# Output stage in two phases: all merges by 512 tokens, then the last projection by Strassen's block product

## The chip, the cores and the metric

One core of one Trainium2 chip runs the whole program. The metric is the time of one execution on the device, in microseconds. TensorE (PE) multiplies matrices into PSUM; VectorE (DVE), ScalarE (ACT) and GpSimd (POOL) work on SBUF tiles of 128 partitions, and SyncE (SP) issues most DMA transfers. Each engine runs its instructions in the order in which they were fixed when the program was built, and waits for the others by semaphores.

## The reference

One layer with two mixers in parallel over 2048 latent tokens of width 1024, in fp32. The change lies in what follows the mixers:

```
ya = rmsnorm(oa, gla_onorm).reshape(b, t, GLA_V) * jax.nn.silu(ag)
yb = rmsnorm(ob, gdn_onorm).reshape(b, t, GDN_V) * jax.nn.silu(bg)
gates = jax.nn.sigmoid(mg + b_gate.astype(jnp.float32))
merged = gates[..., :D_MODEL] * jnp.matmul(ya, w_gla_out) + gates[..., D_MODEL:] * jnp.matmul(yb, w_gdn_out)
out_x = jnp.matmul(merged, w_o)
...
x = x + (gt_x[:, None, :] * out_x).astype(dtype)
return rmsnorm(x, final_g)
```

`ya` and `yb` are 2048 x 512 each, `w_gla_out` and `w_gdn_out` 512 x 1024, `w_o` 1024 x 1024.

## The kernel before

**Products.** An fp32 operand is kept as two tiles of the type fp32r, a rounded half `h` and the rest `l`. `split` makes them: a cast on ScalarE (L132) and a subtraction on VectorE or GpSimd (L135, after the argument `lo`). A product is three matmuls for each 128 rows of depth: h·h, h·l and l·h.

**Blocks.** The latent tokens are 8 blocks of 256 (two tiles of 128), finished by the scans in the order 3, 4, 2, 5, 1, 6, 0, 7. Gated mixer outputs lie in DRAM as `d_y`, gates as `d_gate`. The output stage has two parts for each block.

`out_merge(b)` (from L1579) makes `merged` for 256 tokens, transposed: for each of 8 column tiles j, 12 matmuls of 128 x 256 for either mixer into the two halves of one PSUM bank `pm` (L1592), 192 a block. VectorE then computes (stored gate + 1) · pm (L1596), adds the two mixers (L1598), and `split` makes `mh` (ScalarE) and `ml` (VectorE). Its weights `wab` are split in `out_weights`; the raw tiles `wr` come from a ring of four.

`phase_out` (from L1603) does the last projection: for each token tile and half of the 1024 columns 24 matmuls of 128 x 512 into `pz` (L1661), 96 a block, against `wo`, the whole of `w_o` in halves, in SBUF. Then VectorE multiplies by `gtb` (L1666), GpSimd adds x (L1667), and ScalarE squares and sums (L1668). `flush` finishes a tile a little later: the inverse root on GpSimd (L1631, L155, L156), the scaling on VectorE (L1635), and the store (L1637). The y of the next block is loaded and split (`out_y`, on ScalarE and GpSimd) while a block's projection runs.

**What sets the order.** The code calls `out_merge` and the projection by turns, block by block; the build keeps each engine's order by data dependences and its priorities. For block 3, the weights and merges are woven into the last step of the scans (`phase_mix`, L1519 to L1521), together with that step's remaining matmuls (L1409 among them); `w_o` is split there and in the first block's projection. PSUM has two banks for `pm`; `mt`, the tile behind a merge and a projection, is one buffer.

## Time and profile before

| | |
|---|---|
| runs, us | 2157.18, 2164.18, 2164.04 (median 2164.04) |
| profiled execution's own time, us | 2161.12 |
| its span in the profile, us | 2159.3 |
| granted TensorE clock over the span | 0.989 |
| output stage alone, from the end of the scans' matmuls, us of the span | 1813.4 to 2159.3 |

The span is the time from the first to the last instruction that the profile shows; the execution's own time holds what lies around it as well. Lines named L1592 and the like are lines of the kernel before unless the text says that they are of the changed one. In rows of the trace `out<-in` gives the tiles by the program's names, then the shape, and in brackets how long the engine had been idle and what ended that.

### The profile page before, as it was taken

Reading aid. Unit: us, or ns where it says so; the run is one execution under the profiler, and the core shown is the slowest. Engines: PE = TensorE matmul, PEld = TensorE weight load, DVE = VectorE, ACT = ScalarE, POOL = GpSimd, SP = SyncE. Lnnn points to the kernel's source line nnn. Section 1 sums busy time; section 2 is a strip of 40 time slices with the busy share of each in tenths; the row PEclk is TensorE's granted clock in tenths of the full one; section 3 lists DMA queues with packets and bytes.
Section 4 is the critical chain, followed back from the end, with each engine's and each line's share of the span. In section 5 each row is a group of like instructions: output and inputs, shape, how many; then the busy total and the mean of one; then the engine's idle time right before and its main releaser. Section 6 shows DMA issues by size and latency. Waiting matters only on the chain.

```text
span 2159.3 us, 41811 instructions
## 1 busy us (share of the span) xinstructions
PE 2062.3 (96%) x16096; PEld 1730.3 (80%) x16096; DVE 1215.5 (56%) x2185; ACT 899.0 (42%) x2212; POOL 858.6 (40%) x779
## 2 busy tenths in 40 slices
PE   5999999999999999999999999899988888999998
PEld 2688888888888888777777777788888777999888
DVE  3813555556777553556555555566677776444333
ACT  4644255555452223443434443355555554112111
POOL 2410122222221015666666663456566664222331
...
GB/s 288 104 86 116 50 69 64 63 62 72 61 62 80 71 80 133 138 138 152 143 127 148 128 142 140 262 286 292 308 281 288 285 212 273 130 134 114 98 88 79
DMA packets 275012, 315.60 MB, mean 146 GB/s; under 512 B 22280, under 2 KB 206844, under 8 KB 274812
## 3 DMA queue, kind: packets, MB, share of 16 engines
...
q14 instruction: 73, 0.60, 0.1%
HBM read 203.00 MB, written 109.84 MB: 145 GB/s over the span
## 4 chain that ended last, share of the span: by engine, by line
PE 82%; DVE 5%; ACT 5%; DMA 3%; POOL 2%; issue 2%; SPq 1%; DVEq 0%; POOLq 0%; ACTq 0%
PE pz L371 46%; PE pz L1661 8%; PE pm L1592 8%; DMA g<-dg 2%; PE pe L936 1%; PE pe L1118 1%; PE pl L995 1%; PE pl L988 1%; PE pl L996 1%; PE pz L1080 1%; DVE ql L1215 1%; ACT E L1209 1%; PE pz L1059 1%; PE pq L614 1%; PE pz L1347 1%
## 5 line engine op out<-in xcount | busy, mean ns | idle before, releaser
L371 PE MATMUL pz<-hi,wh 128*128 128x512 f32 (+1 forms) x1560 | 621.6, 399 | 1.5 <-DVE hi L134 1.5
L371 PE MATMUL pz<-lo,wh 128*128 128x512 f32 (+1 forms) x1560 | 600.3, 385 | 1.8 <-POOL lo L135 1.8
L371 PE MATMUL pz<-hi,wl 128*128 128x512 f32 (+1 forms) x1520 | 588.4, 387 | 0.0
L371 PEld LDWEIGHTS pz<-lo,wh 128*128 128x128 f32 x1560 | 294.7, 189 | 51.0 <-POOL lo L135 3.6
L371 PEld LDWEIGHTS pz<-hi,wh 128*128 128x128 f32 x1560 | 294.3, 189 | 47.8 <-DVE hi L134 2.4
L371 PEld LDWEIGHTS pz<-hi,wl 128*128 128x128 f32 x1520 | 286.1, 188 | 53.9 <-issue 0.4
L135 POOL TENSOR_TENSOR wl<-w,wh 128x1024 fp32r<-128x1024 f32 x44 | 110.0, 2500 | 437.5 <-ACT wh L132 312.0
L569 DVE SCALAR_TENSOR_TENSOR acc<-zpad,cw,acc 128x1024 f32<-128x1024 f32 x192 | 272.3, 1418 | 6.6
L1592 PE MATMUL pm<-yh,wab 128*128 128x256 f32 x1024 | 188.2, 285 | 2.2 <-ACT fsq L1402 1.4
L873 DVE CAST_PREDICATED U<-kit,pl 128x256 f16<-128x256 int32 x216 | 91.1, 431 | 139.2 <-PE pl L996 135.4
L1592 PEld LDWEIGHTS pm<-yh,wab 128*128 128x128 f32 x1024 | 161.8, 193 | 3.1 <-ACT fsq L1402 1.6
L1661 PE MATMUL pz<-wo,mh 128*128 128x512 f32 (+1 forms) x528 | 161.3, 388 | 0.0
L1592 PE MATMUL pm<-yl,wab 128*128 128x256 f32 x512 | 145.5, 284 | 0.0
L989 ACT CAST ppb<-pl 128x256 f16<-128x256 f32 x216 | 73.5, 373 | 166.7 <-PE pl L988 160.3
L1216 POOL TENSOR_TENSOR E<-E,ak 128x256 f32<-128x256 f32 x96 | 78.9, 841 | 110.6 <-ACT E L1209 67.0
L1661 PEld LDWEIGHTS pz<-wo,mh 128*128 128x128 f32 x528 | 98.2, 189 | 20.1
L135 DVE TENSOR_TENSOR sql<-sq,sqh 128x512 fp32r<-128x512 f32 (+1 forms) x36 | 28.0, 804 | 140.5 <-ACT sqh L132 140.2
L624 POOL TENSOR_TENSOR acc<-acc,sq 128x512 f32<-128x512 f32 x32 | 50.6, 1586 | 137.7 <-ACT sq L623 77.7
L1661 PE MATMUL pz<-wo,ml 128*128 128x512 f32 (+1 forms) x264 | 102.0, 386 | 0.0
L1592 PEld LDWEIGHTS pm<-yl,wab 128*128 128x128 f32 x512 | 98.9, 193 | 0.3
L135 POOL TENSOR_TENSOR yl<-wr,yh 128x1024 fp32r<-128x1024 f32 x16 | 39.2, 2462 | 128.2 <-ACT yh L132 128.2
L1666 DVE TENSOR_TENSOR mt<-pz,gtb 128x512 f32<-128x512 f32 (+1 forms) x33 | 22.3, 675 | 115.3 <-PE pz L1661 113.1
...
## 6 DMA issues: line engine op xcount, KB each, us to landing
...
dqkv<-acc SPq DMA_DIRECT2D x192, 64.0 KB, 1.6
...
```

The lines of the kernel that those rows point to most:

```text
L135: getattr(nc, lo).tensor_tensor(dst_lo, src, dst_hi.bitcast(F32), op=ALU.subtract)
L371: nc.tensor.matmul(ps[:, 0:n], a[:, kk, :], b[:, kk, :], start=(k == 0), stop=(k == last - 1))
L569: nc.vector.scalar_tensor_tensor(acc, src, wcol, acc, op0=ALU.mult, op1=ALU.add)
L614: nc.tensor.matmul(u[4][:, 0:u[2]], self.ones, u[3][i], start=(i == 0), stop=(i == 1))
L624: nc.gpsimd.tensor_tensor(v, v, r, op=ALU.mult)
L873: self.nc.vector.copy_predicated(out, mv, data)
L936: nc.tensor.matmul(ps[:, o + a * P:o + 256], qk[:, 1, h, :], kq[:, h, a:2, :], start=True, stop=True)
L989: nc.scalar.copy(ppl, pc.rearrange("p h (j i) -> p h j i", i=m))
L1216: nc.gpsimd.tensor_tensor(E[:, :, li, 1], E[:, :, li, 1], k, op=ALU.mult)
L1592: nc.tensor.matmul(ps[:, half * 256:half * 256 + 256], wab[wi][:, k, j * P:(j + 1) * P], yy[:, k, :], start=(i == 0), stop=(i == 11))
L1661: nc.tensor.matmul(ps, aa[:, k, i * P:(i + 1) * P], wo[k][wi][:, cs], start=(j == 0), stop=(j == 23))
L1666: nc.vector.tensor_tensor(sq, ps, gtb[:, cs], op=ALU.mult)
```

## The change

The output stage becomes two phases.

*Merges first.* Blocks are taken in four groups of two (`groups`), and each merge matmul moves 512 tokens (L1597 of the changed kernel, 192 a group). The product with the gate is now one L1600 for each mixer, then one addition (L1604); the result is stored to DRAM (`d_m`, L1605), with no split. The group's y are four tiles (hi and lo for each mixer). `out_weights` keeps `wab` in four pairs of columns.

*w_o.* It is no longer kept whole. During the last merge group and after it, `wo_block` makes seven blocks of 512 x 512 in halves: B11, B21 and B22 themselves, T1 = B12 - B11, T3 = B22 - B12 (one subtraction, L1624), T2 = B22 - T1 and T4 = B21 - T2 (two subtractions, of the hi and of the lo half, L1629).

*The product.* Each block of 256 tokens by 1024 is cut into A11 to A22 (128 tokens by 512). `m_raws` reads it back, `m_sums` makes S1 = A21 + A22, S2 = S1 - A11, S3 = A22 - S2, S4 = A12 - S2 on VectorE (L1643), and `m_halves` splits each left operand (cast on ScalarE; subtraction on VectorE for even products, on GpSimd for odd ones; four buffers). Seven products of 12 matmuls of 128 x 512 (L1738) replace 96 matmuls with 84. Products 2, 4 and 6 (counted from 0) accumulate onto the bank of product 0, product 5 onto that of product 1. ScalarE copies the bank after products 0, 1, 2 and 4 (L1743); VectorE (L1752, L1758) and GpSimd (L1755) add what makes the four quarters of the output. `fin` does what followed the projection before (L1725 on VectorE, L1726 on GpSimd, L1727 on ScalarE), four times a block, and `flush` the end of a tile (L1704, L155, L156 on GpSimd, L1708 on VectorE). The sums and splits of the next block's first three products are made during products 4 to 6.

```diff
-NW = 6
...
+PRODUCTS = (("A11", "B11"), ("S1", "T1"), ("S2", "T2"), ("A12", "B21"), ("S3", "T3"), ("S4", "B22"), ("A22", "T4"))
...
+        self.d_m = dp.tile([NLAT // 2, P, 8, 256], F32, name="dm")
...
-                gens.append((itertools.chain(self.out_weights(), self.out_merge(self.blocks[0])), 10))
+                gens.append((itertools.chain(self.out_weights(), self.out_merge(0)), 10))
...
-    blocks = (3, 4, 2, 5, 1, 6, 0, 7)
+    groups = ((3, 4), (2, 5), (1, 6), (0, 7))
 
     def out_open(self):
-        wp = self.pool("owa", 1, side="right")
-        self.yp = self.pool("oy", 1, side="right")
-        self.sp = self.pool("os", 2, side="right")
+        self.bp = self.pool("ob", 1, side="right")
+        self.sp = self.pool("os", 3, side="right")
         self.pm = self.pool("opm", 2, PSUM, side="right")
-        self.wab = [wp.tile([P, 8, D], F32R, name=f"wab{i}") for i in range(2)]
+        self.wab = [[self.w_blk().rearrange("p a b -> p (a b)").rearrange("p (k n) -> p k n", k=8) for _ in range(2)]
+                    for _ in range(4)]
...
-    LO = ("vector", "gpsimd") * 7 + ("vector", "vector")
+    LO = ("vector", "gpsimd")
...
+    def out_y(self, g):
+        pool = (self.bp, self.yp)[g % 2] if g else self.bp
+        self.y2 = [pool.tile([P, 4, 512], F32R, name=f"y{i}") for i in range(4)]
+        for e in range(2):
+            for hf in range(2):
+                cs = slice(256 * e, 256 * e + 256)
+                raw = self.yraw.pop(0) if self.yraw else self.y_raw(self.groups[g][e], hf)
+                self.split(self.y2[hf][:, :, cs], self.y2[2 + hf][:, :, cs], raw, lo=self.LO[hf])
+
+    def out_merge(self, g):
+        nc, y = self.nc, self.y2
+        b0, b1 = self.groups[g]
+        bs = slice(b0, b1 + 1, b1 - b0)
+        pair = lambda t: t.rearrange("p (e t) -> p e t", e=2)
         for j in range(8):
...
+            gs = []
+            for i in range(2):
+                ga = self.sp.tile([P, 512], F32, name="ga")
+                nc.sync.dma_start(pair(ga), self.d_gate[bs, :, 8 + 8 * i + j, :].rearrange("b p t -> p b t"))
+                ps = self.pm.tile([P, 512], F32, name="pm")
+                n = 0
+                for k in range(4):
+                    for wi, yy in ((0, y[i]), (0, y[2 + i]), (1, y[i])):
+                        nc.tensor.matmul(ps, self.wab[j // 2][wi][:, 4 * i + k, (j % 2) * P:(j % 2) * P + P],
+                                         yy[:, k, :], start=(n == 0), stop=(n == 11))
+                        n += 1
+                nc.vector.scalar_tensor_tensor(ga, ga, 1.0, ps, op0=ALU.add, op1=ALU.mult)
+                gs.append(ga)
+                if i == 0:
+                    yield
+            nc.vector.tensor_tensor(gs[0], gs[0], gs[1], op=ALU.add)
+            nc.sync.dma_start(self.d_m[bs, :, j, :].rearrange("b p t -> p b t"), pair(gs[0]))
+            yield
...
+    def wo_block(self, name, hi, lo):
+        nc = self.nc
+        for e in range(2):
+            ks = slice(2 * e, 2 * e + 2)
+            if name[0] == "B":
+                x = self.wo_piece(int(name[1]) - 1, int(name[2]) - 1, e)
+            elif name in ("T1", "T3"):
+                a, b = ((0, 1), (0, 0)) if name == "T1" else ((1, 1), (0, 1))
+                x, y = self.wo_piece(*a, e), self.wo_piece(*b, e)
+                nc.vector.tensor_tensor(x, x, y, op=ALU.subtract)
+            else:
+                o = self.wo["T1" if name == "T2" else "T2"]
+                x = self.wo_piece(1, 1 if name == "T2" else 0, e)
+                for t in o:
+                    nc.vector.tensor_tensor(x, x, t[:, ks].bitcast(F32), op=ALU.subtract)
+            self.split(hi[:, ks], lo[:, ks], x, lo=self.LO[e])
+        self.wo[name] = (hi, lo)
+
+    def m_raws(self, b):
+        m = []
+        for h in range(2):
+            t = self.w_raw().rearrange("p (k t) -> p k t", k=4)
+            self.nc.sync.dma_start(t, self.d_m[b][:, 4 * h:4 * h + 4])
+            m.append(t)
+        return {f"A{i + 1}{h + 1}": m[h][:, :, i * P:i * P + P] for i in range(2) for h in range(2)}
+
+    def m_sum(self, w, nm, a, b, op):
+        w[nm] = w[b] if nm == "S4" else self.mp.tile([P, 4, P], F32, name="r0" if nm in ("S1", "S3") else "r1", bufs=1)
+        self.nc.vector.tensor_tensor(w[nm], w[a], w[b], op=op)
+
+    def m_sums(self, w, part):
+        if part == 0:
+            self.m_sum(w, "S1", "A21", "A22", ALU.add)
+            self.m_sum(w, "S2", "S1", "A11", ALU.subtract)
+        else:
+            self.m_sum(w, "S3", "A22", "S2", ALU.subtract)
+            self.m_sum(w, "S4", "A12", "S2", ALU.subtract)
+
+    def m_halves(self, w, p):
+        hi, lo = (self.mp.tile([P, 4, P], F32R, name=n, bufs=self.NHL) for n in ("hi", "lo"))
+        self.split(hi, lo, w[PRODUCTS[p][0]], lo=self.LO[p % 2])
+        w[p] = (hi, lo)
+
+    NHL = 4
...
+            xp = self.pool("ox", 3, ctx=ctx)
+            self.mp = self.pool("om", 1, ctx=ctx)
+            self.yp = self.pool("oy1", 1, ctx=ctx)
+            self.sp = self.pool("og", 4, ctx=ctx)
...
+            for g in range(1, 4):
+                gen = self.out_merge(g)
+                if g < 3:
+                    y = self.y2
+                    self.out_y(g + 1)
+                    nxt, self.y2 = self.y2, y
+                    for _ in gen:
+                        pass
+                    self.y2 = nxt
+                    continue
+                self.wo_block("B11", *yt(self.bp, 0))
+                self.wo_block("T1", *yt(self.bp, 1))
+                for n, _ in enumerate(gen):
+                    if n in (3, 7, 11):
+                        self.wo_block({3: "T2", 7: "B21", 11: "T3"}[n], self.w_blk(), self.w_blk())
+            w = self.m_raws(order[0])
+            self.m_sums(w, 0)
+            for p in range(3):
+                self.m_halves(w, p)
+            self.m_sums(w, 1)
+            self.wo_block("B22", self.w_blk(), self.w_blk())
+            self.wo_block("T4", *yt(self.yp, 0))
...
+            for bi, b in enumerate(order):
+                end = bi + 1 == len(order)
+                nw = None if end else self.m_raws(order[bi + 1])
+                xs = []
+                for i in range(2):
+                    x = xp.tile([P, D], F32, name="x")
+                    nc.sync.dma_start(x, io["x"][0, (2 * b + i) * P:(2 * b + i + 1) * P, :])
+                    xs.append((x, xp.tile([P, 2], F32, name=f"oss{i}")))
+                tile_ = lambda: self.sp.tile([P, 512], F32, name="ga")
+
+                def fin(s, src, i, h, last=False):
+                    x, ss = xs[i]
+                    cs = slice(512 * h, 512 * h + 512)
+                    nc.vector.tensor_tensor(s, src, gtb[:, cs], op=ALU.mult)
+                    (nc.vector if last else nc.gpsimd).tensor_tensor(x[:, cs], x[:, cs], s, op=ALU.add)
+                    nc.scalar.activation(s, x[:, cs], AF.Square, accum_out=ss[:, h:h + 1])
+
+                for p, (_, r) in enumerate(PRODUCTS):
+                    if p in (0, 1, 3):
+                        ps = self.pv()
+                        a, c = (ps if p == 0 else a), (ps if p == 1 else None if p == 0 else c)
+                    else:
+                        ps = c if p == 5 else a
+                    k = 0
+                    for kk in range(4):
+                        for u, v in ((0, 0), (0, 1), (1, 0)):
+                            nc.tensor.matmul(ps, w[p][u][:, kk, :], self.wo[r][v][:, kk, :],
+                                             start=(k == 0 and p in (0, 1, 3)), stop=(k == 11), skip_group_check=True)
+                            k += 1
+                    if p in (0, 1, 2, 4):
+                        s = tile_()
+                        nc.scalar.copy(s, ps)
+                    if p == 0:
+                        s1 = s
+                        flush()
+                    elif p == 1:
+                        s5 = s
+                    elif p == 2:
+                        s2 = s
+                    elif p == 3:
+                        nc.vector.tensor_tensor(s1, ps, s1, op=ALU.add)
+                        fin(s1, s1, 0, 0)
+                    elif p == 4:
+                        nc.gpsimd.tensor_tensor(s, s, s5, op=ALU.add)
+                        fin(s, s, 1, 1)
+                    elif p == 5:
+                        nc.vector.tensor_tensor(s2, ps, s2, op=ALU.add)
+                        fin(s2, s2, 0, 1)
+                        pend.append((2 * b, *xs[0]))
+                    else:
+                        if end:
                             flush()
...
+                        fin(tile_(), ps, 1, 0, end)
+                        pend.append((2 * b + 1, *xs[1]))
+                    if p < 4:
+                        self.m_halves(w, p + 3)
+                    elif nw is not None:
+                        self.m_halves(nw, p - 4)
+                    if nw is not None and p in (3, 6):
+                        self.m_sums(nw, 0 if p == 3 else 1)
+                w = nw
+            flush(2)
```

Three places show how the engines' orders change. The first is VectorE in the steady part: before, the four projections of one block and the start of the next block's merges.

```order
L1666 TENSOR_TENSOR mt<-pz,gtb 128x512 x3
L1635 SCALAR_TENSOR_TENSOR xo<-xo,rsq,fgb 128x1024
L1666 TENSOR_TENSOR mt<-pz,gtb 128x512
L1596 SCALAR_TENSOR_TENSOR mt<-ga,pm 128x512
L1598 TENSOR_TENSOR mt<-mt 128x256
L135 TENSOR_TENSOR ml<-mt,mh 128x256
```

Of the changed kernel, VectorE over one block of the loop (`lo` are splits, `r_...` are sums S, `ga` with `pz` the output quarters; the split of an A reads the raw tile `wr`):

```order
L135 TENSOR_TENSOR lo<-wr,hi 128x512
L1752 TENSOR_TENSOR ga<-pz,ga 128x512
L135 TENSOR_TENSOR lo<-wr,hi 128x512
L1725 TENSOR_TENSOR ga<-ga,gtb 128x512 x2
L1643 TENSOR_TENSOR r_22923<-wr,r_22859 128x512
L1758 TENSOR_TENSOR ga<-pz,ga 128x512
L135 TENSOR_TENSOR lo<-r_22859,hi 128x512
L1725 TENSOR_TENSOR ga<-ga,gtb 128x512
L1643 TENSOR_TENSOR r_22859<-wr,r_22859 128x512
L1725 TENSOR_TENSOR ga<-pz,gtb 128x512
L1708 SCALAR_TENSOR_TENSOR x<-x,rsq,fgb 128x1024 x2
L135 TENSOR_TENSOR lo<-r_22923,hi 128x512
```

Where VectorE had four gate products and one scaling between merges, it now has, in one row of dependences, sums and splits of the next block among the four output quarters of this one.

GpSimd at the same place: before, the splits of the next y, then one tile's additions of x and its inverse root; the second tile's follow alike.

```order
L135 TENSOR_TENSOR yl<-wr,yh 128x1024 x2
L1667 TENSOR_TENSOR xo<-xo,mt 128x512 x2
L1631 TENSOR_TENSOR oss<-oss 128x1
L155 TENSOR_SCALAR rsq<-oss 128x1
L156 TENSOR_TENSOR rsq<-rsq,mhalf 128x1
```

Of the changed kernel, one block:

```order
L1726 TENSOR_TENSOR x<-x,ga 128x512
L1755 TENSOR_TENSOR ga<-ga 128x512
L135 TENSOR_TENSOR lo<-r_23193,hi 128x512
L1726 TENSOR_TENSOR x<-x,ga 128x512 x2
L1704 TENSOR_TENSOR oss_23100<-oss_23100 128x1
L1726 TENSOR_TENSOR x<-x,ga 128x512
L135 TENSOR_TENSOR lo<-wr,hi 128x512
L1704 TENSOR_TENSOR oss_23103<-oss_23103 128x1
L155 TENSOR_SCALAR rsq<-oss_23103 128x1
L155 TENSOR_SCALAR rsq<-oss_23100 128x1
L156 TENSOR_TENSOR rsq<-rsq,mhalf 128x1 x2
L135 TENSOR_TENSOR lo<-r_23195,hi 128x512
```

Additions of the quarters and splits now stand between the additions of x; two roots come together after the last one.

ScalarE at the same place is the second: before, the squares of one block, the casts of `mh` in the next merges and those of the next y.

```order
L1668 ACTIVATE mt,oss<-xo 128x512 x4
L132 CAST mh<-mt 128x256 x7
L132 CAST yh<-wr 128x1024 x2
L132 CAST mh<-mt 128x256
L1668 ACTIVATE mt,oss<-xo 128x512 x4
```

Of the changed kernel, one block, from the copy of product 2 to that of the next block's product 0:

```order
L1743 COPY ga<-pz 128x512
L132 CAST hi<-wr 128x512
L1727 ACTIVATE ga,oss_23100<-x 128x512
L1743 COPY ga<-pz 128x512
L132 CAST hi<-r_23193 128x512
L132 CAST hi<-r_23195 128x512
L1727 ACTIVATE ga,oss_23103<-x 128x512
L1727 ACTIVATE ga,oss_23100<-x 128x512
L132 CAST hi<-wr 128x512
L1727 ACTIVATE ga,oss_23103<-x 128x512
L132 CAST hi<-r_23259 128x512
L1743 COPY ga<-pz 128x512
```

The copy of the next block's product 0 (`COPY ga<-pz`, the last row) now stands behind the square of this block's last quarter and the cast of S3 (`r_23259`).

The third place is VectorE in the last merge group. Before, the pieces of `w_o` were split during the first block:

```order
L135 TENSOR_TENSOR ml<-mt,mh 128x256
L1596 SCALAR_TENSOR_TENSOR mt<-ga,pm 128x512
L135 TENSOR_TENSOR wo_21403<-wr,wo_21402 128x1024
L1598 TENSOR_TENSOR mt<-mt 128x256
L135 TENSOR_TENSOR ml<-mt,mh 128x256
L1596 SCALAR_TENSOR_TENSOR mt<-ga,pm 128x512
```

Of the changed kernel, the beginning of the last group (`wr<-wr` are differences, `y_...` and `wb` their halves):

```order
L1604 TENSOR_TENSOR ga<-ga 128x512
L1600 SCALAR_TENSOR_TENSOR ga<-ga,pm 128x512
L1624 TENSOR_TENSOR wr<-wr 128x1024
L1600 SCALAR_TENSOR_TENSOR ga<-ga,pm 128x512
L1629 TENSOR_TENSOR wr<-wr,y_22059 128x1024
L1604 TENSOR_TENSOR ga<-ga 128x512
L1629 TENSOR_TENSOR wr<-wr,y_22060 128x1024
L1600 SCALAR_TENSOR_TENSOR ga<-ga,pm 128x512
L1629 TENSOR_TENSOR wr<-wr,y_22059 128x1024
L1629 TENSOR_TENSOR wr<-wr,y_22060 128x1024
L1600 SCALAR_TENSOR_TENSOR ga<-ga,pm 128x512
L135 TENSOR_TENSOR wb<-wr,wb 128x1024
```

Differences and splits of 1024 columns now stand between one merge's L1600 and the next, on the engine that empties the merges' banks.

131 lines of the change are left out of this document (33 added, 98 removed).

## The prediction

> **What bounds the kernel now.** I began with the page: how busy each engine is, and which engine the chain that ended last runs through.
>
> ```profile
> span 2159.3 us, 41811 instructions
> PE 2062.3 (96%) x16096; PEld 1730.3 (80%) x16096; DVE 1215.5 (56%) x2185; ACT 899.0 (42%) x2212; POOL 858.6 (40%) x779
> PE 82%; DVE 5%; ACT 5%; DMA 3%; POOL 2%; issue 2%; SPq 1%; DVEq 0%; POOLq 0%; ACTq 0%
> ```
>
> These are averages over the program; the change touches its last 400 us alone. So I followed the chain of waits there (start us, us, what).
>
> ```profile
> 1798.05 9.08 PE pm L1592 x72
> ...
> 1809.13 3.62 issue
> 1812.75 0.65 PE pe L1409 x4
> 1813.41 22.91 PE pz L1661 x93
> 1836.31 23.04 PE pm L1592 x192
> 1859.35 22.03 PE pz L1661 x96
> ...
> 2129.75 22.27 PE pz L1661 x120
> 2152.02 0.03 issue
> ```
>
> From 1813 on, TensorE is the whole chain: 23.04 us of merges and 22.03 us of projection in turn, without a gap. A merge matmul with 256 moving columns takes 23.04/192 = 120 ns, one with 512 columns 22.03/96 = 229.5 ns. The other engines follow it. Ahead of that lie short waits; of TensorE's waits between 1755 and 1840 (total, times, longest) two are the merges' own:
>
> ```profile
> PE pm L1592 <- ACT fsq L1402: 1.4, 1, 1.4
> PE pm L1592 <- DVE mt L1596: 0.8, 1, 0.8
> ```
>
> **What comes off TensorE.** All merges were 1536 matmuls of 256 columns (8 x 23.04 us) and become 768 of 512 columns (8 x 96 x 0.2295 = 8 x 22.03 us): **-8.1 us**. The projection goes from 96 to 84 matmuls of 512 columns a block, 22.03 to 19.28 us: 8 x 2.75 = **-22.0 us**. The early waits, 3.62 + 1.4 + 0.8 = 5.8 us, came from the last scan step, weight splits and first merges sharing queues. They are not tied to the new order, but a merge of 512 columns now waits for y of two blocks. I take **-4 us** (bounds 0 and, with the slow clock shown below, -7.5).
>
> **What the new loop costs.** TensorE needs 19.28 us a block, so the question is whether VectorE, GpSimd and ScalarE can keep that pace. The costs of their work, from rows of the same operations and shapes (ns min/median/max):
>
> ```profile
> L1666 DVE TENSOR_TENSOR mt<-pz,gtb x33: 424/691/692, 1824.9 to 2152.1; 128x512 f32<-128x512 f32 x31, 128x256 f32<-128x256 f32 x2
> L135 DVE TENSOR_TENSOR lo<-hf,hi x18: 676/691/693, 36.8 to 112.6; 128x512 fp32r<-128x512 f32 x18
> L1635 DVE SCALAR_TENSOR_TENSOR xo<-xo,rsq,fgb x17: 746/1277/2295, 1831.8 to 2155.5; 128x1024 f32<-128x1024 f32 x15, 128x512 f32<-128x512 f32 x2
> L1667 POOL TENSOR_TENSOR xo<-xo,mt x30: 1280/1292/2267, 1825.7 to 2141.6; 128x512 f32<-128x512 f32 x30
> L135 POOL TENSOR_TENSOR lo<-hf,hi x18: 1267/1338/1735, 35.2 to 109.0; 128x512 fp32r<-128x512 f32 x18
> L132 ACT CAST sqh<-sq x36: 406/614/625, 261.5 to 635.0; 128x512 fp32r<-128x512 f32 x32, 128x256 fp32r<-128x256 f32 x4
> ```
>
> Per block VectorE has 3 operations of 512 columns with one input in PSUM, L1752, L1758 and one L1725 (2.1 us), 11 with both in SBUF, four L1643, four L135 and three L1725 (7.6 us), and two L1708 (2.55 us): 12.2 us. GpSimd has five additions (6.5), three L135 (4.0) and two inverse roots (about 2): 12.5 us. ScalarE has four copies and seven casts (6.8) and four squares (2.9): 9.7 us. Each alone fits in 19.28. But VectorE and GpSimd don't run beside each other freely. The timeline (start us, us) shows it:
>
> ```profile
> 1875.98 0.69 DVE L1666 TENSOR_TENSOR mt<-pz,gtb 128x512 f32<-128x512 f32 x1 [4.81 <-PE pz L1661]
> 1876.59 1.27 DVE L1635 SCALAR_TENSOR_TENSOR xo<-xo,rsq,fgb 128x1024 f32<-128x1024 f32 x1
> ...
> 1876.75 2.26 POOL L1667 TENSOR_TENSOR xo<-xo,mt 128x512 f32<-128x512 f32 x1 [2.28 <-DVE mt L1666]
> ...
> 1882.26 1.29 POOL L1667 TENSOR_TENSOR xo<-xo,mt 128x512 f32<-128x512 f32 x1 [3.25 <-DVE mt L1666]
> ...
> 1860.52 4.95 POOL L135 TENSOR_TENSOR yl<-wr,yh 128x1024 fp32r<-128x1024 f32 x2 [20.09 <-ACT yh L132]
> ...
> 1861.72 1.48 DVE L135 TENSOR_TENSOR ml<-mt,mh 128x256 fp32r<-128x256 f32 x1 [1.19 <-ACT mh L132]
> ```
>
> The GpSimd addition that met L1635 took 2.26 us instead of 1.29 and ended at 1879.01, 1.15 after L1635's end (1877.86). A 256-column split that met a GpSimd split (the first of two in 4.95, so until about 1863.0) ended at 1863.20, 0.2 behind it, less than its free 0.42: for 512 columns I take 0.55 of the free 0.69. So a two-input VectorE operation and a GpSimd one take turns. Taken in turn, 7.6 + 2.55 + 6.5 + 4.0 = 20.6 us a block, more than TensorE's 19.28, before any dependence is counted. [...]
>
> Now the dependences, from the order of the instructions. VectorE, GpSimd and ScalarE are in order, so they form a ring through one block. Three more prices: VectorE's back-to-back step is 1876.59 - 1875.98 = 0.61; the rest are
>
> ```profile
> 1873.37 0.19 POOL L1631 TENSOR_TENSOR oss<-oss 128x1 f32<-128x1 f32 x1 [0.83 <-ACT mt L1668]
> ...
> 1873.92 0.55 POOL L156 TENSOR_TENSOR rsq<-rsq,mhalf 128x1 f32<-128x1 f32 x1
> ...
> 1866.99 0.63 ACT L1668 ACTIVATE mt<-xo 128x512 f32<-128x512 f32 x1 [5.30 <-POOL xo L1667]
> 1867.53 0.19 ACT L1668 ACTIVATION_READ_ACCUMULATOR mt<-xo 128x1 f32 x1
> ```
>
> that is 1.1 us from L1631 to the end of L156 (1.4 with the second L155 now between them), and 0.73 for a square with its sum. From the start of L1752, with hand-overs of 0.04 to 0.08:
>
> - L1752, split of A11, L1725 on VectorE: 1.9. GpSimd's L1726: 3.3. ScalarE's square, then the copy of product 4 that stands behind it: 4.7.
> - GpSimd's L1755 needs that copy: 6.0. Its split of the next S1 follows: 7.3, and VectorE's L1725 of product 4 is held until then: 7.9; S3: 8.5.
> - GpSimd's next L1726, held until S3 is done: 9.65. VectorE does L1758 meanwhile; its split of S2 is held: 10.2; L1725 10.8; S4 11.4.
> - L1726 of product 5: 12.6; square 13.35; L1704 13.6; L1726 of product 6 14.9; split of A12 16.2; L1704, both L155 and the first L156 17.6.
> - VectorE's L1708 18.95; GpSimd's split of S4, held, 20.1; the second L1708 21.2; then the split of S3, S1, S2 and the split of A22, 4 x 0.61: **23.7**, and the next L1752 can start.
>
> So a block takes 23.7 us and not 19.28; TensorE would wait some 4.4 us. It shows ahead of the third product, which accumulates onto the bank that ScalarE's copy of the first must have read, and that copy stands behind the square of product 6 (which needs 14.9) and the cast of S3. That is one pause of 3.5 to 4 us and a shorter one ahead of the last product. Seven rings between eight blocks give 7 x 4.4 = 30.9; the last block has no next one to prepare, and I take 2 us for it: **+32.9 us**. In before this cover was ample: two tiles' output work lay beside 45 us of matmuls.
>
> **The last merge group.** By the order of instructions, VectorE has inside it 16 L1600 (0.687 each by L1596's row below, 11.0), 8 L1604 and 6 operations of 512 columns for the first block's sums and splits (14 x 0.69 = 9.7), and 12 of 1024 columns for w_o's differences and splits; GpSimd has five splits of 1024 columns and one of 512.
>
> ```profile
> L135 DVE TENSOR_TENSOR wo<-wr,wo x5: 1216/1224/1858, 1791.6 to 1820.9; 128x1024 fp32r<-128x1024 f32 x5
> L135 POOL TENSOR_TENSOR yl<-wr,yh x16: 2352/2399/2587, 1768.7 to 2088.2; 128x1024 fp32r<-128x1024 f32 x16
> L1596 DVE SCALAR_TENSOR_TENSOR mt<-ga,pm x64: 674/687/691, 1780.5 to 2129.8; 128x512 f32<-128x512 f32 x64
> ```
>
> 11.0 + 9.7 + 12 x 1.224 + 5 x 2.399 + 1.34 = 48.7 us in turns against 44.06 of matmuls: **+5 us** with rounding up for unevenness (bounds 0, if GpSimd's part lies beside L1600, and 13, if w_o's pieces also come late). L1600 itself reads PSUM and is not held. What hid w_o's preparation before was the mixed first block, whose waits I have counted.
>
> **The end.** Before, 2159.3 - 2152.0 = 7.3 us followed the last matmul. Now its last tile has 512 columns where it had 256 (about +1), the other tile's L1708 in two halves comes in between, and the ring is still 2 to 3 us behind: **+4 us** (bounds +1 and +6). The merged values now go through DRAM (eight writes of 256 KB a group, two reads of 512 KB a block). Each block's are read some ten microseconds or more after the last of them was written, and the DMA engines had room (their share stands ahead of the GB/s):
>
> ```profile
> 1840.00:1860.00 20.00, 20.00 (x166) 19.87 (x165) 11.79 (x22) 3.46 (x8) 0.43 (x1) 1.00 0.44 145
> ```
>
> I cost it at nothing (bounds 0 and the 8 us of late pieces in the last merge group, the one place where w_o's pieces come on top).
>
> **Sum.** -8.1 - 22.0 - 4 + 32.9 + 5 + 4 = +7.8. The profiled execution took 2161.1 us of its own, so about 2169; the median of the three runs is 2.9 us above that execution, their mean 0.7, and I put the forecast between, at **2170 us**. Some 30 us saved on TensorE come back as waits for the engines behind it.
>
> **The rivals.**
>
> *The ring is hidden* (the other side: faster). If GpSimd and VectorE overlapped, the ring loses its holds: 1.3 at the split of S1, 0.5 at S2's, about 1.2 at L1708, so 20.7; and the last merge group, 35 us of VectorE, hides wholly. Then 8 x 1.4 + 4 - 34.1 = -19, **2142**; with the ring below 19.28, 2131. It decides at 19.28 us a block. For it speaks that no engine is above 12.5 us; against it the 2.26 beside the 1.29. Chance 0.17, at 2137. *Half of the holds* are missed by luck of the phases: 22.2 a block, 12 us less, **2158**: 0.10.
>
> *The slow clock.* The windows (us, busy of PE, PEld, DVE, ACT and POOL, then the granted clock) show what the 3.62 us pause did:
>
> ```profile
> 1811.00:1813.00 2.00, 0.25 (x2) 0.28 (x3) 1.91 (x4) 0.13 (x1) 1.80 (x1) 1.00 0.51 174
> 1813.00:1814.00 1.00, 1.00 (x6) 0.87 (x5) 1.00 (x2) 0.13 (x1) 0.56 (x1) 0.61 0.87 286
> 1814.00:1815.00 1.00, 1.00 (x4) 0.74 (x3) 1.00 (x3) 0.58 (x2) 0.00 (x0) 0.50 0.66 200
> 1815.00:1816.00 1.00, 1.00 (x4) 0.81 (x3) 1.00 (x2) 0.74 (x1) 0.13 (x1) 0.50 0.60 181
> 1816.00:1817.00 1.00, 1.00 (x4) 0.76 (x4) 0.15 (x1) 0.00 (x0) 1.00 (x1) 0.68 0.89 269
> ```
>
> Right after it the clock was 0.50 for about 3.4 us, 1.7 us lost. The ring's pause is as long. On the ring's scale the square of product 6 ends at 15.7, S3's cast at 16.3 and the copy at 16.9; two products (5.5 us) from there reach 22.5, 1.2 ahead of L1752; so 0.5 to 0.7 of each 1.7 shows, 8 x 0.7 = 5.6 and **2176**. Chance 0.15. [...]
>
> *w_o comes late*: its pieces and the ring of four raw buffers stand in VectorE's order, and a late piece holds the merges' L1600 behind it; 8 us more, **2178**. Chance 0.10. That the count of matmuls doesn't fall is excluded by the code; that it falls and the time doesn't is the forecast.
>
> **How the numbers follow.** Forecast 0.48, alone between 2162 and 2180. A measurement can tell about 0.5%, 10.8 us, so faster is below 2153.2 and slower above 2174.9. Of the forecast's 0.48, 0.33 lies between and 0.15 above; the hidden ring is faster; half of the holds 0.03 faster and 0.07 the same; the slow clock and late w_o slower. Faster 0.20, same 0.40, slower 0.40. The range takes in all but the hidden ring: down to 2158 less the early waits' and the end's bounds (6.5), with a little of that rival's side, 2148, and up to 2178 with the clock's 5.6 and the end's 2 together, 2188.
>
> **What would show it.** Right: blocks of 22.5 to 24 us in the loop, a pause of 3.5 to 4 us ahead of every third product put down to ScalarE's copy L1743, GpSimd operations of over 2 us or VectorE ones of over 1 us beside each other; merges of 44 us a group in the second and third, 49 or more in the last. Wrong: blocks of 19.3 us, or operations of 0.69 and 1.29 side by side undisturbed.

## The result, and the profile after

| | before | changed |
|---|---|---|
| runs, median us | 2161.97 (2157.18 to 2164.18, 4 runs) | 2189.07 (2187.09 to 2189.57, 4 runs) |
| ratio | | 1.0127, interval 1.0106 to 1.0147 |
| profiled execution's own time, us | 2161.12 | 2187.09 |
| span, us | 2159.3 | 2185.1 |

The change makes the kernel 1.3% slower. TensorE has fewer matmuls to do, 15208 where it had 16096, and lost more in waits than it saved. The page of the changed kernel, its span, its busy times and its chain by engine:

```profile
span 2185.1 us, 40275 instructions
PE 2056.3 (94%) x15208; PEld 1680.2 (77%) x15208; DVE 1275.7 (58%) x2188; ACT 927.4 (42%) x2240; POOL 901.8 (41%) x807
PE 70%; DMA 9%; DVE 8%; ACT 5%; POOL 4%; issue 3%; SPq 1%; DVEq 0%; POOLq 0%; ACTq 0%
```

The chain ran 82% through TensorE before, 70% now; DMA has gone from 3 to 9%, VectorE from 5 to 8. TensorE's waits in the three stretches 1765:1845, 1845:1930 and 1930:2195 (total, times, longest) show for whom:

```profile
PE pm L1597 <- DVE ga L1600: 3.6, 3, 1.9
PE pe L1409 <- POOL og L1405: 2.5, 1, 2.5
PE pm L1597 <- DVE y L135: 2.3, 1, 2.3
...
PE pm L1597 <- DVE ga L1600: 1.5, 1, 1.5
...
PE pz L1738 <- ACT ga L1743: 21.5, 9, 4.5
PE pm L1597 <- DVE ga L1600: 8.4, 7, 2.9
```

The last two carry most: 21.5 us in the loop of block products, 8.4 in the last merge group.

**Where an execution stood when the output stage began.** The scans ahead of the change end at slightly different times from run to run, so stages are compared from the same instruction, the last scan step's L1357 on VectorE. Before and of the changed kernel (start us, us):

```profile
1757.12 1.28 DVE L1357 TENSOR_TENSOR og<-og,pz 128x512 f32<-128x512 f32 x2 [1.25 <-PE pz L1347]
```

```profile
1756.19 1.28 DVE L1357 TENSOR_TENSOR og<-og,pz 128x512 f32<-128x512 f32 x2 [1.25 <-PE pz L1347]
```

From there to the end of the span it was 2159.3 - 1757.1 = 402.2 us, and is 2185.1 - 1756.2 = 428.9: 26.7 more. The forecast, on the same measure, was 402.2 + 7.8 = 410.0. It falls into three stages, whose borders are the first block product on TensorE (1982.0) and the end of its last matmul (2173.6):

| stage | forecast, us | measured, us | off by |
|---|---|---|---|
| L1357 to the first block product (merges) | 211.6 | 225.8 | +14.2 |
| loop of block products | 187.1 | 191.6 | +4.5 |
| after the last matmul | 11.3 | 11.5 | +0.2 |

**The loop.** One block of the chain of waits in the changed kernel (start us, us, what; short links left out):

```profile
2046.24 0.69 DVE ga L1752
...
2048.22 1.29 POOL x L1726
...
2050.81 1.29 POOL ga L1755
...
2052.13 1.77 DVE ga L1725
...
2055.10 1.10 DVE lo L135
...
2056.87 1.67 POOL x L1726
...
2059.58 1.23 POOL x L1726
...
2061.55 0.51 ACT hi L132
2062.06 0.49 ACT ga L1743
...
2062.60 7.43 PE pz L1738 x24
...
2070.05 0.69 DVE ga L1752
```

This is the forecast's ring, link by link: L1725 and the split held behind GpSimd (1.77 and 1.10 instead of 0.69), L1726 held behind VectorE (1.67 instead of 1.29), the cast of S3, the copy. It takes 2070.05 - 2046.24 = 23.81 us. One link differs: from the copy on, the chain goes through TensorE's products 2 and 3, which take 7.43 us and not 5.5. The windows behind the same pause one block earlier (busy PE, PEld, DVE, ACT, POOL; granted clock) say why:

```profile
2037.00:2039.00 2.00, 0.20 (x1) 0.20 (x2) 0.00 (x0) 1.97 (x5) 1.76 (x4) 1.00 0.00 0
2039.00:2040.00 1.00, 1.00 (x4) 0.81 (x4) 0.41 (x1) 0.76 (x2) 1.00 (x2) 0.73 0.00 0
2040.00:2041.00 1.00, 1.00 (x4) 0.72 (x3) 1.00 (x2) 0.00 (x0) 1.00 (x2) 0.50 0.00 0
2041.00:2042.00 1.00, 1.00 (x4) 0.81 (x3) 1.00 (x1) 0.00 (x0) 1.00 (x1) 0.50 0.29 119
2042.00:2043.00 1.00, 1.00 (x4) 0.79 (x3) 1.00 (x1) 0.00 (x0) 0.01 (x1) 0.57 0.99 406
```

Behind the pause the granted clock is halved (0.50), as in before behind its 3.62 us wait.

**The merges.** TensorE's row in the merge stage (start us, us; idle before it and what ended that in brackets; only starts after a wait are shown):

```profile
1777.89 5.06 PE L1597 MATMUL pm<-y,wb 128*128 128x512 f32 x11 [2.29 <-DVE y L135]
...
1805.02 3.06 PE L1597 MATMUL pm<-y,wb 128*128 128x512 f32 x12 [1.44 <-DVE ga L1600]
1809.93 12.78 PE L1597 MATMUL pm<-y,wb 128*128 128x512 f32 x48 [1.86 <-DVE ga L1600]
...
1896.69 35.75 PE L1597 MATMUL pm<-y,wb 128*128 128x512 f32 x156 [1.53 <-DVE ga L1600]
...
1942.27 6.09 PE L1597 MATMUL pm<-y,wb 128*128 128x512 f32 x24 [2.86 <-DVE ga L1600]
1949.88 11.27 PE L1597 MATMUL pm<-y,wb 128*128 128x512 f32 x48 [1.51 <-DVE ga L1600]
```

There are waits at the start, one in the third group, and a train of them in the last, whose 192 matmuls take some 55 us (from about 1926.9 to 1982.0) where the matmuls alone are 44.06. Ahead of the wait in the third group VectorE stood 3.51 us for a late piece of w_o, in front of the L1600 that frees the bank:

```profile
1894.82 1.22 DVE L1624 TENSOR_TENSOR wr<-wr 128x1024 f32<-128x1024 f32 x1 [3.51 <-DMA wr<-in_w_o]
1895.96 0.68 DVE L1600 SCALAR_TENSOR_TENSOR ga<-ga,pm 128x512 f32<-128x512 f32 x1
```

What VectorE was doing before 1942.27:

```profile
1935.64 0.68 DVE L1600 SCALAR_TENSOR_TENSOR ga<-ga,pm 128x512 f32<-128x512 f32 x1
1936.46 1.22 DVE L1629 TENSOR_TENSOR wr<-wr,y 128x1024 f32<-128x1024 f32 x1
1937.61 2.88 DVE L1604 TENSOR_TENSOR ga<-ga 128x512 f32<-128x512 f32 x1
1940.41 1.21 DVE L1629 TENSOR_TENSOR wr<-wr,y 128x1024 f32<-128x1024 f32 x1
1941.54 0.67 DVE L1600 SCALAR_TENSOR_TENSOR ga<-ga,pm 128x512 f32<-128x512 f32 x1
```

Between two L1600, each of which empties a bank, stand two of w_o's differences and an addition that is held for 2.88 us; GpSimd's split of T1 ran from 1936.88 for 3.05.

### The profile page after: what moved, and what is told of

Its sections match the earlier page's. It is cut to its first block, busy times and chain, and to the rows that moved or that the text cites. A ratio compares the mean times of both kernels' runs of the same rounds, so it can differ in the third digit from the quotient of the medians.

```text
span 2185.1 us, 40275 instructions
## 1 busy us (share of the span) xinstructions
PE 2056.3 (94%) x15208; PEld 1680.2 (77%) x15208; DVE 1275.7 (58%) x2188; ACT 927.4 (42%) x2240; POOL 901.8 (41%) x807
## 4 chain that ended last, share of the span: by engine, by line
PE 70%; DMA 9%; DVE 8%; ACT 5%; POOL 4%; issue 3%; SPq 1%; DVEq 0%; POOLq 0%; ACTq 0%
PE pz L371 45%; PE pm L1597 3%; PE pz L1738 2%; DMA g<-dg 2%; DMA ga<-dgate 2%; PE pe L936 1%; POOL x L1726 1%; PE pl L995 1%; PE pl L988 1%; PE pe L1118 1%; PE pl L996 1%; DMA wr<-in_w_o 1%; DMA dm<-ga 1%; PE pz L1080 1%; DVE ga L1725 1%
## 5 line engine op out<-in xcount | busy, mean ns | idle before, releaser
L1597 PE MATMUL pm<-y,wb 128*128 128x512 f32 x768 | 185.1, 400 | 15.9 <-DVE ga L1600 13.5
L1597 PEld LDWEIGHTS pm<-y,wb 128*128 128x128 f32 x768 | 145.2, 191 | 53.7 <-DVE ga L1600 17.5
L1738 PE MATMUL pz<-wb,hi 128*128 128x512 f32 x256 | 88.2, 428 | 17.0 <-ACT ga L1743 17.0
L554 ACT COPY zpad<-pz 128x512 f32<-128x512 f32 x48 | 28.2, 588 | 137.5 <-PE pz L371 137.5
L1118 PE MATMUL pe<-wt,gh 128*128 128x256 f32 x264 | 76.1, 316 | 8.7 <-ACT E L1209 4.7
L1600 DVE SCALAR_TENSOR_TENSOR ga<-ga,pm 128x512 f32<-128x512 f32 x64 | 43.6, 684 | 68.5 <-DMA ga<-dgate 36.5
L135 POOL TENSOR_TENSOR y<-wr,y 128x1024 fp32r<-128x1024 f32 x11 | 29.5, 2692 | 126.2 <-ACT y L132 126.2
L132 ACT CAST y<-wr 128x1024 fp32r<-128x1024 f32 x22 | 22.4, 1045 | 134.8 <-PE pm L1597 105.1
L1738 PEld LDWEIGHTS pz<-wb,hi 128*128 128x128 f32 x256 | 51.8, 205 | 33.1 <-ACT ga L1743 20.5
```

Of the source, the lines that this page charges most:

```text
L135: getattr(nc, lo).tensor_tensor(dst_lo, src, dst_hi.bitcast(F32), op=ALU.subtract)
L554: nc.scalar.copy(zpad[:, 1 + r0:1 + r0 + nr, 1:1 + GW], ps[:, 0:n].rearrange("p (r w) -> p r w", w=GW))
L1118: self.nc.tensor.matmul(out, g[:, i, ct * P:(ct + 1) * P], self.wt[:, d, cols[0]:cols[1]], start=(j == 0), stop=(j == 1))
L1597: nc.tensor.matmul(ps, self.wab[j // 2][wi][:, 4 * i + k, (j % 2) * P:(j % 2) * P + P], yy[:, k, :], start=(n == 0), stop=(n == 11))
L1600: nc.vector.scalar_tensor_tensor(ga, ga, 1.0, ps, op0=ALU.add, op1=ALU.mult)
L1738: nc.tensor.matmul(ps, w[p][u][:, kk, :], self.wo[r][v][:, kk, :], start=(k == 0 and p in (0, 1, 3)), stop=(k == 11), skip_group_check=True)
```

## The experiments

Three questions were open: whether the ring of three engines makes the loop (and what in it), what the slow clock adds, and what starves the merges. In the table, "stage" is the span from L1357 to the end; "last group" is TensorE's waiting for L1600 from 1930 on; the block is the usual distance of one L1752 to the next (of groups_without_strassen, of one block's matmuls to the next's).

| run | median us | ratio to before (interval) | stage us | block us | last group us |
|---|---|---|---|---|---|
| changed kernel | 2189.07 | 1.0127 (1.0106 to 1.0147) | 428.9 | 23.8 | 8.4 |
| groups_without_strassen | 2167.89 | 1.0020 (1.0003 to 1.0038) | 406.9 | 22.4 | 6.9 |
| p4_sum_on_dve | 2182.21 | 1.0085 (1.0066 to 1.0104) | 418.3 | 22.5 and 23.1 | 8.5 |
| lo_all_dve | 2177.65 | 1.0063 (1.0048 to 1.0078) | 418.5 | 21.8 and 23.2 | 6.9 |
| p4_and_lo_dve | 2160.77 | 0.9985 (0.9972 to 0.9997) | 401.0 | 20.4 | 8.2 |
| filler_in_pause | 2186.66 | 1.0098 (1.0081 to 1.0115) | 424.6 | 23.35 | 8.4 |
| m_store_on_act | 2204.39 | 1.0191 (1.0172 to 1.0210) | 445.8 | 22.4 to 24.9 | 9.1 |
| m_store_from_y | 2188.68 | 1.0110 (1.0095 to 1.0125) | 428.2 | 23.8 | 10.0 |
| wo_no_subtract | 2182.03 | 1.0095 (1.0069 to 1.0121) | 418.8 | 23.8 | 5.7 |
| wo_lo_dve | 2153.62 | 0.9958 (0.9940 to 0.9977) | 393.9 | 20.4 | 4.2 |
| m_own_buffers | 2166.19 | 1.0009 (0.9994 to 1.0024) | 401.0 | 20.4 | 7.7 |
| all_three | 2157.05 | 0.9968 (0.9955 to 0.9981) | 393.1 | 20.4 | 2.6 |
| y_lo_gpsimd | 2159.56 | 0.9966 (0.9951 to 0.9980) | 395.7 | 20.4 | 4.6 |

**groups_without_strassen.** The merges as in the changed kernel, then the plain product of w_o's four quarters.

```diff
-PRODUCTS = (("A11", "B11"), ("S1", "T1"), ("S2", "T2"), ("A12", "B21"), ("S3", "T3"), ("S4", "B22"), ("A22", "T4"))
+PRODUCTS = (("A11", 0), ("A12", 0), ("A21", 0), ("A22", 0))
...
+                for q in range(4):
+                    i, h = q // 2, q % 2
+                    ps = self.pv()
+                    k = 0
+                    for kh in range(2):
+                        for kk in range(4):
+                            for u, v in ((0, 0), (0, 1), (1, 0)):
+                                nc.tensor.matmul(ps, w[2 * i + kh][u][:, kk, :], self.wo[f"B{kh + 1}{h + 1}"][v][:, kk, :],
+                                                 start=(k == 0), stop=(k == 23))
+                                k += 1
```

> One part of the change alone: merges in four groups through DRAM as in the changed kernel, then the plain product of four blocks of w_o (96 matmuls a block, no sums, no differences, no copies by ScalarE). Ring theory: this loop has no ring, TensorE bounds it at 22.03 us a block, below the changed kernel's 23.8; merges of the last group within 2 us of 44.06, as only four splits remain there; time 2189 - 8 x 1.8 - 7 - 4 of the end = about 2164, near before. If the merges through DRAM are what costs (rival), it stays above 2175.

2167.89, near the expected 2164: with 96 matmuls a block TensorE doesn't wait in this loop at all, and 22.4 us is shorter than the 23.8 that 84 matmuls take with their ring. So the block product as written costs more than the matmuls it saves. The stage is still 4.7 us longer than before (406.9 to 402.2). 3.1 us of that is the loop, whose matmuls take 233 ns where the projection's took 229 (179.4 us for 8 x 22.03); up to the first of them it is 219.6 us, where all but the projection and the end took 218.7 before (402.2 - 8 x 22.03 - 7.3). So the merges in groups don't bring the 8.1 us that their matmuls save; in the last group TensorE waits 6.9 us even without any difference of w_o, and not the 2 expected.

**p4_sum_on_dve, lo_all_dve, p4_and_lo_dve.** These take links out of the ring: product 4's sum (copy on ScalarE and L1755 on GpSimd become one operation of VectorE), GpSimd's three splits, and both.

```diff
-                    if p in (0, 1, 2, 4):
+                    if p in (0, 1, 2):
...
-                        nc.gpsimd.tensor_tensor(s, s, s5, op=ALU.add)
+                        s = tile_()
+                        nc.vector.tensor_tensor(s, ps, s5, op=ALU.add)
```

```diff
-        self.split(hi, lo, w[PRODUCTS[p][0]], lo=self.LO[p % 2])
+        self.split(hi, lo, w[PRODUCTS[p][0]], lo="vector")
```

> The sum of product 4 is made by VectorE straight from PSUM; ScalarE's copy of product 4 and GpSimd's L1755 go. Ring theory: copy, L1755 and the hold of L1725 behind GpSimd's split leave the ring, 23.8 becomes about 21 us a block and the pause ahead of product 2 about 1.5 us; time 2189 - 7 x 2.8 = about 2169. Rival, that a pause before product 2 is ScalarE's own queue (square of product 6, cast of S3, then the copy) whatever stands ahead on VectorE and GpSimd: 0.6 us less a block at most, 2185.

> All splits of left operands in the loop are subtracted by VectorE; GpSimd's three a block (1.34 us each) go, VectorE has three more (0.61 each). Theory of taking turns: the ring loses what VectorE waits behind GpSimd's splits, 4.0 - 1.8 = 2.2 us, 23.8 becomes about 21.7 a block and the time about 2189 - 7 x 2.1 = 2174. Rival, that VectorE's own row of instructions is the bound: blocks of 24.5 or more, 2194. Rival, that the pause before product 2 with the slow clock behind it (7.4 us for two products instead of 5.5) sets the block: no change, 23.8 and 2189, unless the pause falls below about 1.8 us.

> Both edits: product 4's sum straight from PSUM on VectorE, and all left splits on VectorE. GpSimd keeps the four additions of x and the roots. Theory of taking turns: turns a block are 11 + 3 two-input operations at 0.61, two L1708 and four additions of 1.29, 8.5 + 2.5 + 5.2 = 16.2 us, below TensorE's 19.28; blocks of 20 us or less and a time near 2189 - 7 x 3.8 = 2162. If the queue of ScalarE before product 2 (squares, casts, copy) is the ring by itself: 22 to 23 as with the first edit alone, 2180.

Each alone brings about 10.5 us of stage, both 27.9. Of lo_all_dve's 10.4, 5.6 lie ahead of the first L1752 and not in the ring. The first edit alone fell short of its expectation (21 us a block, 2169); its time is nearer to that of the rival named there, 2185. VectorE got more work by the second edit and the loop got shorter: its row is not the bound. The turns with GpSimd are, or GpSimd's own row, which the edit shortens as well; these two are not told apart here. With one edit alone the pause ahead of product 2 is still 1.6 to 2.7 us, and the blocks come in two lengths. VectorE's L1752 in lo_all_dve:

```profile
2023.32 0.69 DVE L1752 TENSOR_TENSOR ga<-pz,ga 128x512 f32<-128x512 f32 x1 [1.25 <-PE pz L1738]
2045.16 0.68 DVE L1752 TENSOR_TENSOR ga<-pz,ga 128x512 f32<-128x512 f32 x1
2068.32 0.69 DVE L1752 TENSOR_TENSOR ga<-pz,ga 128x512 f32<-128x512 f32 x1 [1.25 <-PE pz L1738]
```

and the granted clock in the second half of these two blocks (the third number from the end):

```profile
2033.00:2045.00 12.00, 10.19 (x44) 7.87 (x43) 7.97 (x11) 5.19 (x12) 4.74 (x8) 1.00 0.28 93
...
2055.00:2068.00 13.00, 10.99 (x41) 8.45 (x40) 8.05 (x11) 4.78 (x11) 4.74 (x8) 0.87 0.31 115
```

At full clock the block is 21.84 us, as the theory of turns had it (21.7); where the clock fell it is 23.16. With both edits the pause is 0.6 to 0.7 us, the clock is 1.00 in the windows from 2098 to 2118, and blocks are 20.4 us from the second on (the first still takes 23.0, with a wait of 3.2 us ahead of product 6):

```profile
2078.27 0.68 DVE L1752 TENSOR_TENSOR ga<-pz,ga 128x512 f32<-128x512 f32 x1
2098.64 0.69 DVE L1752 TENSOR_TENSOR ga<-pz,ga 128x512 f32<-128x512 f32 x1
```

**filler_in_pause.** Twelve more matmuls behind product 1, whose result nothing reads.

```diff
+                    if p == 1:
+                        d = self.pm.tile([P, 512], F32, name="pm")
+                        for k in range(12):
+                            nc.tensor.matmul(d, w[1][0][:, 0, :], self.wo["T1"][0][:, 0, :], start=(k == 0), stop=(k == 11))
```

> Adds 12 matmuls of 512 columns (2.75 us) into an unused bank of pm behind product 1 in each block, whose result nothing reads, so that TensorE is not idle in the 3.2 to 4.5 us ahead of product 2. If the slow clock is on the ring (products 2 and 3 at half clock end 1.9 us later and L1752 waits for them): blocks get shorter, 23.8 to 22 or 23.4 (the VectorE row), time 2175 to 2186, although TensorE does 12 matmuls more a block. If the slow clock lies beside the ring: 23.8 stays, 2189. If the fillers hold TensorE up: 24 or more.

The pause shrinks from about 2.5 to 0.4 us, and products 2 and 3 follow at full clock (1.00 in the windows from 2050 to 2090). The block gets shorter by 0.45 us although it has twelve matmuls more (L1756 is this kernel's L1752):

```profile
2027.95 0.68 DVE L1756 TENSOR_TENSOR ga<-pz,ga 128x512 f32<-128x512 f32 x1
2051.30 0.68 DVE L1756 TENSOR_TENSOR ga<-pz,ga 128x512 f32<-128x512 f32 x1
```

So the ring that closes in VectorE's own row, without products 2 and 3, is 23.35 us, and of the 1.7 us that the slow clock takes from these products (the windows from 2039 to 2043 above), 0.45 shows. The median moved by 2.4 us (8 x 0.45 = 3.6).

**m_store_on_act, m_store_from_y, m_own_buffers.** Three trials on the path of m: another queue for its store, a store of equal size from a tile of y (the output is then not the kernel's), and tiles of its own for the sum in groups 1 to 3, on top of p4_and_lo_dve.

```diff
-            nc.sync.dma_start(self.d_m[bs, :, j, :].rearrange("b p t -> p b t"), pair(gs[0]))
+            nc.scalar.dma_start(self.d_m[bs, :, j, :].rearrange("b p t -> p b t"), pair(gs[0]))
```

```diff
-            nc.sync.dma_start(self.d_m[bs, :, j, :].rearrange("b p t -> p b t"), pair(gs[0]))
+            nc.sync.dma_start(self.d_m[bs, :, j, :].rearrange("b p t -> p b t"), pair(y[0][:, 0, :].bitcast(F32)))
```

```diff
-            nc.vector.tensor_tensor(gs[0], gs[0], gs[1], op=ALU.add)
-            nc.sync.dma_start(self.d_m[bs, :, j, :].rearrange("b p t -> p b t"), pair(gs[0]))
+            m = self.xp.tile([P, D], F32, name="x")[:, 0:512] if g else gs[0]
+            nc.vector.tensor_tensor(m, gs[0], gs[1], op=ALU.add)
+            nc.sync.dma_start(self.d_m[bs, :, j, :].rearrange("b p t -> p b t"), pair(m))
```

> Only the store of m (L1605) is issued by ScalarE instead of SyncE, so that loads of the gates no longer stand behind it in one queue. Queue theory: SyncE's waits at L1605 (38.8 us) and at the gate loads behind it go, the first group loses its waits for L1600 (3.6 us and a stretch at half clock) and the loop starts 5 to 10 us earlier than 1982, near 1974; time about 2181. Rival, that a gate's buffer is the limit (it comes free only when the store has landed, 4.6 us, whatever queue issued it) or VectorE: the loop starts within 2 us of 1982 and the time stays near 2189. The loop's blocks stay at 23.8 either way.

> The store to m's place takes the same number of bytes from a tile of y instead of the sum, so the output differs; the same traffic, but a gate's buffer comes free when the addition L1604 is done and not when the store has landed. Buffer theory of the merges: TensorE's waits for L1600, 3.6 us in the first group, 1.5 in the second and third and 8.4 in the last, fall to under 4 us in all, and the loop starts at 1973 or before instead of 1982; time about 2180. Rival, that the DMA engines' load or VectorE's work is what delays: the waits stay above 10 us in all and the loop starts within 2 us of 1982.

> On top of p4_and_lo_dve: in groups 1 to 3 the sum of a merge goes to tiles of its own (those of x, idle in this phase) and is stored from there, so a gate's buffer is free after L1604. Output complete. Buffer theory: SyncE's waits for the store of m fall from 65.8 to below 25 us, TensorE's waits in groups 1 to 3 from 9.7 to under 6, time about 2156. Rival, as the run with the store from y already suggests: TensorE's waits change by under 2 us and the time stays at 2160.

The profile had suggested this path, and misled. SyncE's waits from 1775 to 1985, first of p4_and_lo_dve, then of m_own_buffers:

```profile
SPq L1592 <- DMA dm<-ga: 65.8, 27, 4.9
```

```profile
SPq L1606 <- DVE x L1605: 62.1, 21, 6.5
...
SPq L1592 <- DMA dm<-ga: 10.7, 6, 3.9
```

55 us of SyncE's waiting for the store went (its wait moved to the store itself), and the stage stayed at 401.0 (the median is 5 us higher, and the profiled execution had reached L1357 4.6 us later). The changed kernel's store from y did the same: 428.2 to 428.9. So taking the store's landing and the gates' buffers out of SyncE's waits doesn't move the end, and they are not what starves the merges. The other queue made it worse by 17 us, which neither side of its expectation had: a gate's load then took 4.9 us to land in the median where it took 3.4, the waits for L1600 grew in every group, from 13.5 to 20.8 us in all, and the granted clock from 1775 to 1985 was 0.94 in the mean where it was 0.98. Why loads land later beside stores of another queue wasn't tried.

**wo_no_subtract, wo_lo_dve, all_three.** The last merge group: w_o's differences left out, so that the output is not the kernel's; all of w_o's splits on VectorE, on top of p4_and_lo_dve; and that together with m_own_buffers.

```diff
-                nc.vector.tensor_tensor(x, x, y, op=ALU.subtract)
...
-                for t in o:
-                    nc.vector.tensor_tensor(x, x, t[:, ks].bitcast(F32), op=ALU.subtract)
```

```diff
-            self.split(hi[:, ks], lo[:, ks], x, lo=self.LO[e])
+            self.split(hi[:, ks], lo[:, ks], x, lo="vector")
```

> Leaves out the subtractions that make T1 to T4 (the pieces are still loaded and split), so the output differs. VectorE theory for the last merge group: eight operations of 1.22 us go from it, 48.7 us of turns become 38.9, below 44.06, and TensorE's 8.4 us of waits in that group fall to under 2; the loop starts near 1975 and the time is about 2182. Rival, that the pieces of w_o and the gates arrive late: the waits stay at 6 us or more. The first group's waits and the loop's 23.8 us stay.

> On top of p4_and_lo_dve: the splits of w_o's blocks are subtracted by VectorE alone, so the five GpSimd operations of 2.4 us in the last merge group go and VectorE has five of 1.22 more. Theory of taking turns: the additions L1604 that stood 2.8 us behind such a split take 0.69 again; turns in the group fall from 48.7 to about 42.7 us, TensorE's waits for L1600 there from 8.2 to under 4.5 us; time about 2156. Rival, that late pieces of w_o and late gates make those waits: they stay at 7 us or more and the time at 2160.

> p4_and_lo_dve, wo_lo_dve and m_own_buffers together. If both causes add: waits of the merges in groups 1 to 3 under 4 us in all, time about 2152, some 0.5% faster than before. If only one counts: 2156. If neither: 2160.

Without the differences 5.7 of 8.4 us of waits remain, so their 9.8 us of VectorE work are not the main cause of these waits, against the expectation. The expected time, 2182, came true all the same, by another way: the stage is 10.1 us shorter, of which the last group's waits are only 2.7. The loop starts 6.0 us earlier after L1357 (219.8 for 225.8) and is 4.1 us shorter, 3.6 of it ahead of its first L1752, which no longer stands behind T4's differences. With GpSimd's five splits moved to VectorE, which gives it more work, 8.2 become 4.2, and the additions are no longer held. The first L1604 of the last group in p4_and_lo_dve, then in wo_lo_dve:

```profile
1935.97 2.88 DVE L1604 TENSOR_TENSOR ga<-ga 128x512 f32<-128x512 f32 x1
```

```profile
1936.94 0.69 DVE L1604 TENSOR_TENSOR ga<-ga 128x512 f32<-128x512 f32 x1
```

The stage is 7.1 us shorter than that of p4_and_lo_dve, more than the 4 us of waits in the last group alone: w_o's last blocks are split before the first block products need them (p4_and_lo_dve waited 3.2 us for L1756 in its first block, this one does not). wo_lo_dve is the fastest of all in the median, 0.42% under before. all_three has fewer waits in the last group (2.6) but the same stage within 0.8 us and no better time.

**y_lo_gpsimd.** On top of wo_lo_dve, GpSimd subtracts for the y of the next group, so that those splits leave VectorE's row in the first merge group.

```diff
-                self.split(self.y2[hf][:, :, cs], self.y2[2 + hf][:, :, cs], raw, lo=self.LO[hf])
+                self.split(self.y2[hf][:, :, cs], self.y2[2 + hf][:, :, cs], raw, lo="gpsimd" if g else self.LO[hf])
```

> On top of wo_lo_dve: the y of groups 1 to 3 are subtracted by GpSimd alone, so that VectorE's row in the first merge group holds no split of the next group's y (two of 1.22 us there, one waiting 1.8 us for its cast, one held 0.8 us by GpSimd). If that row makes the first group's waits for L1600 (5.0 us with the stretch at half clock): they fall under 2.5 us and the time to about 2149. If late gates (three buffers in this group, 3.75 us of waiting for a load) or the turns with GpSimd's four splits make them: they stay at 4 us or more and the time at 2153 or above.

The first group's waits fell from 5.0 to 2.7 us, which is on neither side of the expectation, but the one wait in the middle groups grew from 1.8 to 3.7 and the stage is 1.8 us longer. The wait in the middle stands behind 5.04 us in which VectorE waits for a piece of w_o (4.49 in wo_lo_dve), as in the changed kernel. In the first group gates came late: VectorE waited 27.2 us for them from 1775 to 1850 (20.1 in wo_lo_dve), 5.03 for one of them. So what makes the first group slow is not settled.

## Why the prediction was wrong

The forecast was 2170 with a range from 2148 to 2188; no change that can be told and slower had a chance of 0.40 each. It came out at 2189, slower. The mechanism it built on, the ring of three engines, was right; the step that failed is the term for the early waits, a gain of 4 us that did not come, and the terms for the last merge group and the loop's ends were too small.

- **What comes off TensorE: right**, within little. Merge matmuls keep 229 ns (30.02 us for 131 in the chain of the changed kernel); in the loop a product of twelve takes 2.80 us (products start at 1984.77 and 1987.57 in TensorE's row), 233 ns each, so a block's floor is 19.6 us rather than 19.28.
- **The ring: right.** 23.7 was forecast; 23.35 is what VectorE, GpSimd and ScalarE make of it, and the slow clock brings it to 23.8. lo_all_dve, p4_sum_on_dve and p4_and_lo_dve show that the links they take out belong to it. The pause lies where it was put, ahead of product 2 behind the copy L1743, but is 2.45 us in most blocks instead of 3.5 to 4: of the 4.2 us by which a block exceeds its floor, 1.7 are the slow clock behind it. That 23.7 met 23.8 so closely is in part luck, as the ring was put 0.35 too long and the slow clock left out.
- **The slow clock: right in kind and size.** It was a rival for 0.5 to 0.7 us a block and is there with 0.45. It should not have been kept apart from the forecast, since in this kernel the clock fell to 0.50 behind the pause of every block from the third on.
- **The loop's fringes: mis-sized by some 3 us.** The step "Seven rings between eight blocks ... the last block has no next one to prepare, and I take 2 us" put the open end at the wrong side. The last block runs at TensorE's pace from its L1752 on; the first one pays. VectorE's row there:

```profile
1985.81 1.83 DVE L1629 TENSOR_TENSOR wr<-wr,wb 128x1024 f32<-128x1024 f32 x1 [4.45 <-DMA wr<-in_w_o]
...
1993.36 3.55 DVE L1629 TENSOR_TENSOR wr<-wr,wb 128x1024 f32<-128x1024 f32 x2
...
1998.03 0.68 DVE L1752 TENSOR_TENSOR ga<-pz,ga 128x512 f32<-128x512 f32 x1
```

  The first block's product 3 had ended by 1993.2 (four products of 2.80 us from 1982.0); L1752 came 4.8 us later, behind T4's differences, which had waited 4.45 us for a piece of w_o. By the forecast's price four products take 11.0 us, and L1752 came 16.05 us after the first began: 5.0 where 2 had been taken. The other 1.4 of the loop's 4.5 are the seven rings, 23.9 us in the mean (the first 24.42).
- **The last merge group: mis-sized.** The step "+5 us with rounding up for unevenness" set 48.7 us of turns against 44.06 of matmuls. The group took some 55.0 us, 10.9 over its matmuls; 8.4 of that are waits for L1600. The sum of work was not the cause that counts: with 9.8 us of it left out, 5.7 us of waits stay. What counts is where the turns fall: a GpSimd split (2.4 us by its row of before, 3.05 here) holds the addition L1604, which took 2.88 us instead of 0.69, and with it the next L1600 and the bank behind it, and only two banks cover that. Beside it stand late pieces of w_o (VectorE waited 5.9 us for them at L1624 from 1930 on), which the forecast had as a rival of 8 us.
- **The early waits: failed, the largest miss.** The step "I take -4 us" took waits for gone that belonged to queues of before. The new order has its own: from L1357 to the last of the scans' matmuls TensorE waits 12.1 us in all (2.3 of them for y of two blocks, 1.4 and 1.9 for L1600), and it waited 12.2 before, so that none of the 4 us came. Half clock took 7.5 us there where it took 5.1 before (busy time times one minus the granted clock, in windows of 1 us). That makes 6.4 of the 14.2 us by which the merges came late; the last group makes 6.0 of it and the wait in the third 1.5. That y of two blocks must be split before the first merge was named, and the sum still had a gain. Why the new waits are as long as the old ones stays open.
- **The end: right** (+4 forecast, 11.5 - 7.3 = 4.2).
- **The hidden ring** did not come about in this kernel; in p4_and_lo_dve it nearly does (20.4 against a floor of 19.6), which is the point from which that rival was to decide.
